# A hybrid conformer/Mamba-2 layer on one core: stores moved to the GpSimd queue, pair weights loaded wholly from GpSimd, memory pieces handed out by age

## The chip, the cores and the metric

The kernel runs on one core of one Trainium2 chip. The core has TensorE (PE in the profile) for matmuls, VectorE (DVE), ScalarE (ACT), GpSimd (POOL) and SyncE (SP). Each engine works through its own list of instructions in order, and waits at an instruction until the semaphores that it names have come. DMA transfers are issued by SP and by POOL here and run on 16 DMA engines. The metric is the device time of the core in microseconds; lower is better.

## The reference

One layer for two request groups that share weights: 1024 prompt tokens and 32 sample tokens, so 1056 columns in all. Everything is float32.

```
proj = x @ w_in + b_in                      # 1024 -> 11296 columns, split into nine parts
u = a_val * sigmoid(a_glu)                  # branch A: depthwise conv of width 31, layer norm, silu
out_a = (silu(layer_norm(conv31(u))) * silu(a_gate)) @ w_a_out
xbc = silu(conv4(xbc))                      # branch B: x/B/C through a depthwise conv of width 4,
y = ssd_scan(x, dt, A, B, C) + d_skip * x   #           chunked state-space scan, 4 groups of 8 heads
out_b = gated_rmsnorm(y, z) @ w_b_out
merged = sigmoid(g_a) * out_a + sigmoid(g_b) * out_b
x_new = layer_norm(2**0.25 * x + merged @ w_out + sigmoid(g_p) * (p @ w_ple))
```

The new caches (the last 30 and 3 rows of the two convolutions' inputs) and the final scan states are outputs too.

## The kernel before

All activations lie with channels on the 128 partitions and the 1056 tokens along the free dimension. Every matrix product is made of float32r halves: an operand is rounded to a high part by ACT (`..h`) and DVE subtracts to get the low part (`..l`), and three matmuls (high x low, low x high, high x high) give one product.

**Stages.** The work is written as numbered slots, and each slot as a list of named places (`ld0`, `ld`, `st`, `d0`, `a0`, `d1`, `a1`, `a2`, `pm`, `d2`, `pe`, `end`) at which functions registered with `at(slot, place, fn)` run. The order in which the program is written is the order on every engine; no scheduler moves anything.

- Before slot 1: loads, the products with `w_ple`, the `dt` products.
- *Pair slots* 1 to 27 (`pair_slot`): two 128-column tiles of `w_in` at once by a Strassen-like scheme with seven products j = 0 to 6, each 24 matmuls. In the text pair i (0 to 26) is slot i + 1. Its weights are seven 128x512 matrices `w{i}_0` to `w{i}_6`: sums of quarter matrices. A raw tile (`r11`, `r12`, `r22`, `s1`, `s2`, `s3`) is loaded, and for the sums further quarters are added into it by accumulating DMAs that only GpSimd issues (`pw_add`). `s2` gets two additions, is rounded for product 2 (`w{i}_2`), then gets a fourth quarter and is rounded again for product 5 (`w{i}_5`: this is the "S4" of the change). `prep_act(i, pos)` and `prep_dve(i, pos)` say after which product these steps are written. Between them DVE works off a queue of the 31-tap convolution (`run_fill`), as many taps as an estimate of its time allows (`dve[0]` against 2820 ns a product).
- *Classic slots* 28 to 61 (`S_CL` = 28): one 128-column tile of `w_in` each, 72 matmuls, and beside it one step of the state-space scan (`ssd_group`: transposes and products on PE, decay on ACT, carry and updates on DVE). Many tiles are spilled to DRAM and loaded back: `d_z`, `d_yn`, `d_ca`, `d_base`, `d_row`.
- Slots 62 to 77 (`S_OB`, product with `w_b_out`), 78 to 85 (`S_OA`, `w_a_out`), and from 86 (`S_WO`) the product with `w_out`, the last layer norm and the outputs.

**Memory pieces.** Tiles come from two pools of equal pieces, `T` (22 pieces, later more) and `U` (7 slightly longer ones). `tget` takes a piece of `T` if one is free and else one of `U`; `put` appends a piece at the end of its pool's list and `get` takes the head. A piece is put back when the program is written past its last use; the first writer of its next tile waits on the chip until the earlier tile's last reader, a store to DRAM among them, is done.

**Queues.** SP issues all loads and all stores (both through `load`, line 188, and four direct calls), POOL only the accumulating DMAs (line 471). Each DMA takes one of eight semaphores of its queue's kind in turn, so that a DMA may have to wait for the one eight places earlier. All operations of one kind on an engine are recorded at one helper's line: 171 tensor_tensor, 175 scalar_tensor_tensor, 185 activation, 191 matmul, 188 DMA from SP.

Of the kernel before, what the change touches and what calls it, by code (L numbers as in the profile page):

```python
# [102 lines left out]
class Units:  # L103


    def __init__(self, pool, n, cols, prefix):
        self.cols, self.n, self.prefix = cols, 0, prefix
        self.free = deque((pool, f"{prefix}{i}") for i in range(n))
        self.tag = {}

    def get(self, shape, dtype=F32, name="u"):
        assert self.free, f"out of units for {name}"
        tag = self.free.popleft()
        self.n += 1
# [14 lines left out]
def emit(nc, tc, I, O, ctx):  # L129
# [4 lines left out]
    T = Units(tpool, 22, 1064, "t")  # L134
    U = Units(tpool, 7, 1116, "u")
# [51 lines left out]
    def load(dst, src):  # L187
        nc.sync.dma_start(dst, src)  # L188

# [158 lines left out]
    def rstd_chain(get_v, scale, s, done):  # L348
# [21 lines left out]
        def move_row():  # L370
            load(d_row[i:i + 1, :], q["v"][0:1, :])
# [3 lines left out]
        def move_root():  # L375
            load(d_row[i + 1].rearrange("(p c) -> p c", p=96), sm(1))
# [1419 lines left out]
```

## Time and profile before

| | |
|---|---|
| median of 3 runs | 1672.31 us (1670.03 to 1672.37) |
| the profiled execution | 1677.25 us, its span 1675.5 us |
| busy over the span | PE 1541.6 us, DVE 1196.6, ACT 828.6, POOL 120.3 |
| pair slots | about 45 to 654 us |
| classic slots | about 654 to 1261 us |
| products with w_b_out and w_a_out | about 1261 to 1565 us |
| product with w_out, last norm | 1565 us to the end |

Times in the views are microseconds from the start of the span. In the view by stretches a row gives, for each engine, busy time and the number of instructions, then the mean clock granted to TensorE (1.00 is full speed), the busy share of the DMA engines and GB/s. "SPq" is SP issuing a DMA. In the chain of waits a row "DMA a<-b" is the time from a transfer's issue until it landed, where the next step of the chain waited for that landing. Groups carry the program's names with the buffer numbers left out, so `s<-in_w` is any raw `s` tile's load.

### The profile page before, as it was taken

To read this page: it belongs to the slowest core of one execution; us is meant where nothing else is said; L and a number is where in the kernel's file an instruction comes from. 1 tells how busy PE (TensorE), PEld (TensorE's weight loads), DVE (VectorE), ACT (ScalarE), POOL (GpSimd) and SP (SyncE) were. 2 spreads that over 40 slices of the span, in tenths; PEclk is the share of its full clock that TensorE was granted. 3 is DMA by queue.
4 is the path that set the end of the run, shared out by engine and by line. 5 is a ranking of instruction groups with operands and counts; after the bars stand their busy time and mean duration, and the time that the engine had idled before them with its cause. 6 is when DMAs were issued, how large, how long until landed. Compare 5 with 4: busy or idle time off the path is not lost.

```text
span 1675.5 us, 27209 instructions
## 1 busy us (share of the span) xinstructions
PE 1541.6 (92%) x10895; PEld 1487.5 (89%) x10895; DVE 1196.6 (71%) x1628; ACT 828.6 (49%) x1436; POOL 120.3 (7%) x148
## 2 busy tenths in 40 slices
PE   7888899999999998899979897779979999999997
PEld 7888899999999998799979796668969999999997
DVE  7757778888899977998866546545655568686654
ACT  7544343333333345676567566646756344343333
POOL 1211122222122210000000000000000000000000
PEclk9899999999999999999989998899999999999998
DMA  8787778778777862433354545235555546497422
GB/s 292 192 234 168 188 193 206 201 190 227 188 181 168 207 139 63 106 80 96 91 149 107 148 128 145 70 107 149 163 139 160 184 141 218 167 332 247 176 75 82
DMA packets 166205, 272.08 MB, mean 162 GB/s; under 512 B 31607, under 2 KB 87927, under 8 KB 166078
## 3 DMA queue, kind: packets, MB, share of 16 engines
q1 hardware_dynamic: 146638, 234.94, 44.4%
q0 software_dynamic: 19440, 35.40, 13.1%
q8 instruction: 85, 1.39, 0.3%
q14 instruction: 42, 0.34, 0.1%
HBM read 213.07 MB, written 57.22 MB: 161 GB/s over the span
## 4 chain that ended last, share of the span: by engine, by line
PE 61%; DVE 13%; DMA 13%; ACT 7%; issue 4%; SPq 2%; DVEq 0%; ACTq 0%
PE ps L191 60%; SPq L188 2%; DMA d_z<-zt_t 2%; DMA d_ca<-cat_t 2%; DMA d_base<-cb_t 2%; DVE cae_u L175 2%; DVE cao_u L175 2%; DMA out_conv_b<-vin_t 2%; DVE cb_t L175 1%; DMA d_yn<-cbo_t 1%; ACT L_t L185 1%; DMA d_ple<-pl 1%; DMA cw_u<-in_wo 1%; PE ps L974 1%; ACT L185 1%
## 5 line engine op out<-in xcount | busy, mean ns | idle before, releaser
L175 DVE SCALAR_TENSOR_TENSOR cae_u<-uin_u,par,cae_u 128x1086 f32<-128x1086 f32 x120 | 161.1, 1343 | 0.0
L471 POOL DMA_DIRECT2D s<-in_w x135 | 117.4, 997 | 494.1 <-DMA s<-in_w 162.1
L175 DVE SCALAR_TENSOR_TENSOR cao_u<-uin_u,par,cao_u 128x1086 f32<-128x1086 f32 x112 | 150.3, 1342 | 0.0
L185 ACT ACT_TABLE_LOAD x77 | 98.8, 1283 | 58.8 <-DMA d_yn<-cbo_t 24.2
L171 DVE TENSOR_TENSOR wlo<-wraw,whi 128x1024 fp32r<-128x1024 f32 x59 | 72.1, 1223 | 71.5 <-ACT whi L185 71.5
L191 PE MATMUL ps<-L_t,X 128*64 128x128 f32 (+1 forms) x528 | 40.0, 300 | 56.4 <-DVE ps L171 52.9
L191 PEld LDWEIGHTS ps<-L_t,X 128*64 128x64 f32 (+1 forms) x528 | 31.4, 152 | 64.2 <-DVE ps L171 55.7
L185 ACT ACTIVATE whi<-wraw 128x1024 fp32r<-128x1024 f32 x59 | 62.3, 1056 | 47.8 <-PE ps L191 28.3
L175 DVE SCALAR_TENSOR_TENSOR cb_t<-vin_t,par,cb_t 128x1059 f32<-128x1059 f32 x60 | 79.1, 1318 | 3.5 <-ACT cb_t L185 2.3
L175 DVE SCALAR_TENSOR_TENSOR cbo_t<-cbo_t,par,ps 128x128 f32<-128x128 f32 (+1 forms) x144 | 38.7, 331 | 57.2 <-PE ps L191 57.1
L185 ACT ACTIVATE gb_t<-ps,par 128x528 f32<-128x528 f32 x30 | 21.1, 702 | 117.7 <-PE ps L191 111.5
L185 ACT ACTIVATE L_t<-L_t,tk 128x128 f32<-128x128 f32 (+1 forms) x264 | 77.9, 381 | 0.0
L185 ACT ACTIVATE vin_t<-ps,par 128x352 f32<-128x352 f32 (+5 forms) x88 | 38.3, 471 | 62.2 <-PE ps L191 58.3
L191 PE MATMUL ps<-t3l,w_4h 128*128 128x264 f32 x216 | 62.9, 291 | 5.3 <-ACT sg_t L185 5.3
L191 PE MATMUL ps<-t3h,w_4l 128*128 128x264 f32 x216 | 62.9, 291 | 0.0
L171 DVE TENSOR_TENSOR M<-ps,mask 128x128 f32<-128x128 f32 (+1 forms) x36 | 9.9, 274 | 73.9 <-ACT B L185 73.3
L191 PE MATMUL ps<-t3h,w_4h 128*128 128x264 f32 x216 | 62.5, 289 | 0.0
L191 PE MATMUL ps<-n2l,w_2h 128*128 128x264 f32 x216 | 61.7, 286 | 0.2 <-ACT ga_t L185 0.2
L191 PE MATMUL ps<-n2h,w_2h 128*128 128x264 f32 x216 | 61.7, 286 | 0.0
L191 PE MATMUL ps<-t4h,w_6h 128*128 128x264 f32 x216 | 61.6, 285 | 0.0
L191 PE MATMUL ps<-n2h,w_2l 128*128 128x264 f32 x216 | 61.4, 284 | 0.0
L191 PE MATMUL ps<-t4l,w_6h 128*128 128x264 f32 x216 | 61.3, 284 | 0.0
(857 smaller groups left out, 5910.1 us busy)
## 6 DMA issues: line engine op xcount, KB each, us to landing
s<-in_w POOLq DMA_DIRECT2D x135, 256.0 KB, 5.7
r<-in_w SPq DMA_DIRECT2D x81, 256.0 KB, 4.1
s<-in_w SPq DMA_DIRECT2D x81, 256.0 KB, 3.5
wraw<-in_w SPq DMA_DIRECT2D x33, 512.0 KB, 5.7
L_t<-d_accp SPq DMA_DIRECT2D x29, 512.0 KB, 7.0
d_yn<-cbo_t SPq DMA_DIRECT2D x16, 528.0 KB, 8.0
yraw_t<-d_yn SPq DMA_DIRECT2D x16, 528.0 KB, 5.8
wraw<-in_wb SPq DMA_DIRECT2D x16, 512.0 KB, 3.7
```

The costliest lines, as they stand in the source:

```text
L171: nc.vector.tensor_tensor(out, a, b, op)
L175: nc.vector.scalar_tensor_tensor(out, a, s, b, op0, op1)
L185: nc.scalar.activation(out, a, f, **kw)
L188: nc.sync.dma_start(dst, src)
L191: nc.tensor.matmul(out, l, r, start=start, stop=stop, skip_group_check=more)
L471: nc.gpsimd.dma_start(pr[i, n], pw_src(i, (PARTS[n] + ("12",))[k]), accum_op=ALU.add)
L974: nc.tensor.transpose(pX[:nt, j * P:(j + 1) * P], XS[j][:, sl], ident)
```

## The change

1. `store(dst, src, *tiles)` replaces `load` for the stores. In slots below 28 it issues from SP as before; from slot 28 on it issues from GpSimd. It notes which tiles were stored, and puts them back.
2. All raw loads of pair weights (`pw_load`) are issued from GpSimd, in the same queue as the accumulating DMAs. The places in `prep_dve` are rearranged: the load of `s2` moves from position 0 to 3, its first addition from 3 to 5, and loads stand behind additions of the same position.
3. The second rounding of `s2` (product 5) moves: on ACT from position 0 to position 2, on DVE from position 0 to position 3. Product 5 itself stays where it was.
4. `Units` keeps for each free piece the slot in which it was put back, 1.5 slots later for one that was stored in that same slot, and `get` takes the piece with the smallest number. From slot 40 on `tget` compares the oldest of `T` with the oldest of `U`; before that `T` goes first as it did.

```diff
     def put(self, *ts):
         for t in ts:
-            self.free.append(self.tag.pop(id(t))[0])
+            (pool, tag), _ = self.tag.pop(id(t))
+            self.free.append((self.clock[0] + (1.5 if self.stored.pop(id(t), None) == self.clock[0] else 0.0), pool, tag))
     def get(self, shape, dtype=F32, name="u"):
-        tag = self.free.popleft()
+        k = min(range(len(self.free)), key=lambda i: (self.free[i][0], i))
+        _, pool, tag = self.free.pop(k)
...
     def tget(shape=(P, NT), dtype=F32, name="t"):
-        return (T if T.free else U).get(list(shape), dtype, name)
+        old = lambda x: min(f[0] for f in x.free) if x.free else 1e9
+        first = len(T.free) > 0 if cur[0] < S_CL + 12 else old(T) <= old(U)
+        return (T if first else U).get(list(shape), dtype, name)
...
+    def store(dst, src, *tiles):
+        (nc.sync if cur[0] < S_CL else nc.gpsimd).dma_start(dst, src)
+        for x in (T, U):
+            x.stored.update((id(t), cur[0]) for t in tiles)
+        tput(*tiles)
...
     def pw_load(i, n):
-            load(t, pw_src(i, PARTS[n][0]))
+            nc.gpsimd.dma_start(t, pw_src(i, PARTS[n][0]))
...
     def prep_act(i, pos):
-        if pos == 0:
-            pw_hi(i, 5, "s2")
-            pw_hi(i, 6, "r22")
         for j, n in {0: ((0, "r11"),), 2: ((1, "s1"),), 3: ((2, "s2"),), 4: ((3, "r12"),), 5: ((4, "s3"),)}.get(pos, ()):
             pw_hi(i + 1, j, n)
+        if pos == 0:
+            pw_hi(i, 6, "r22")
+        elif pos == 2:
+            pw_hi(i, 5, "s2")
     def prep_dve(i, pos):
         if pos == 0:
-            pw_lo(i, 5, "s2")
-            pw_load(i + 2, "s2")
...
         elif pos == 3:
+            pw_lo(i, 5, "s2")
             pw_lo(i + 1, 1, "s1")
             pw_load(i + 2, "s1")
-            pw_add(i + 2, "s2", 1)
+            pw_load(i + 2, "s2")
...
         elif pos == 5:
             pw_lo(i + 1, 3, "r12")
+            pw_add(i + 2, "s1", 1)
+            pw_add(i + 2, "s2", 1)
             pw_load(i + 2, "r12")
-            pw_add(i + 2, "s1", 1)
...
         def spill():
-            load(d_yn[4 * g + j], XSs[4 * g + j])
-            tput(XSs[4 * g + j])
+            store(d_yn[4 * g + j], XSs[4 * g + j], XSs[4 * g + j])
```

The other stores (`d_row`, `d_ca`, `d_z`, `d_wo`, `d_base`, `d_gate`, the convolution caches, the states) are replaced in the same way. The final output `y` and the stores of `d_ple`, `d_accp`, `d_expa` and `d_dec` stay on SP.

**Place 1: the queues in the middle of the pair slots.** On SP before, about pairs 9 to 11, a stretch in which weight loads (`r`, `s`), input tiles (`uin`, `bt`) and stores (`d_gate`, `d_base`) follow each other:

```order
L188 DMA s_9_2600<-in_w 128x512
L188 DMA uin_u_2604<-in_cache_a 128x30
L188 DMA bt_u_2633<-in_xT 128x1056
L188 DMA bt_u_2635<-in_xT 128x1056
L188 DMA d_gate<-ga_t_2357 128x1056
L188 DMA d_gate<-gb_t_2358 128x1056
L188 DMA s_10_2653<-in_w 128x512
L188 DMA r_10_2684<-in_w 128x512
L188 DMA r_9_2686<-in_w 128x512
```

The same stretch of SP after the change:

```order
L197 DMA uin_u_2604<-in_cache_a 128x30
L197 DMA bt_u_2633<-in_xT 128x1056
L197 DMA bt_u_2635<-in_xT 128x1056
L201 DMA d_gate<-ga_t_2357 128x1056
L201 DMA d_gate<-gb_t_2358 128x1056
L201 DMA d_base<-ga_t_2114 128x1056
L201 DMA d_base<-gb_t_2115 128x1056
L197 DMA bt_t_3121<-d_ple 128x1056
```

And POOL after the change, one pair slot of pair 18 (line 482 is a load, line 487 an addition; the name holds the pair for which the tile is):

```order
L487 DMA s2_19_4946<-in_w1 128x512
L487 DMA s3_19_5048<-in_w1 128x512
L482 DMA r11_20_5119<-in_w1 128x512
L482 DMA r22_19_5121<-in_w1 128x512
L482 DMA s1_20_5189<-in_w1 128x512
L482 DMA s2_20_5191<-in_w1 128x512
L487 DMA s2_19_4946<-in_w1 128x512
L487 DMA s1_20_5189<-in_w1 128x512
L487 DMA s2_20_5191<-in_w1 128x512
L482 DMA r12_20_5257<-in_w1 128x512
L482 DMA s3_20_5287<-in_w1 128x512
```

The six loads of a slot have left SP and stand among the five additions on POOL: eleven issues a slot where there were five.

**Place 2: DVE around the second rounding of `s2`,** pair 20. Before (`w20_5l` is the low part for product 5, `cao`/`cae` are taps of the convolution):

```order
L171 TENSOR_TENSOR w20_5l_5565<-s2_20_5092,w20_5h_5564 128x512
L175 SCALAR_TENSOR_TENSOR cae_u39_4949<-uin_u33_4073,par_74,cae_u39_4949 128x1086
L175 SCALAR_TENSOR_TENSOR cao_u40_5158<-uin_u33_4073,par_74,cao_u40_5158 128x1086
L171 TENSOR_TENSOR w20_6l_5568<-r22_20_5369,w20_6h_5567 128x512
L171 TENSOR_TENSOR w21_0l_5571<-r11_21_5367,w21_0h_5570 128x512
L175 SCALAR_TENSOR_TENSOR cae_u39_4949<-uin_u33_4073,par_74,cae_u39_4949 128x1086
L175 SCALAR_TENSOR_TENSOR cao_u40_5158<-uin_u33_4073,par_74,cao_u40_5158 128x1086
L175 SCALAR_TENSOR_TENSOR cae_u39_4949<-uin_u33_4073,par_74,cae_u39_4949 128x1086
L171 TENSOR_TENSOR w21_1l_5639<-s1_21_5432,w21_1h_5638 128x512
```

After:

```order
L184 SCALAR_TENSOR_TENSOR cae_u39_4948<-uin_u33_4073,par_74,cae_u39_4948 128x1086
L184 SCALAR_TENSOR_TENSOR cao_u40_5155<-uin_u33_4073,par_74,cao_u40_5155 128x1086
L180 TENSOR_TENSOR w20_6l_5568<-r22_20_5364,w20_6h_5567 128x512
L180 TENSOR_TENSOR w21_0l_5565<-r11_21_5362,w21_0h_5564 128x512
L184 SCALAR_TENSOR_TENSOR cae_u39_4948<-uin_u33_4073,par_74,cae_u39_4948 128x1086
L184 SCALAR_TENSOR_TENSOR cao_u40_5155<-uin_u33_4073,par_74,cao_u40_5155 128x1086
L184 SCALAR_TENSOR_TENSOR cae_u39_4948<-uin_u33_4073,par_74,cae_u39_4948 128x1086
L184 SCALAR_TENSOR_TENSOR cao_u40_5155<-uin_u33_4073,par_74,cao_u40_5155 128x1086
L180 TENSOR_TENSOR w20_5l_5636<-s2_20_5191,w20_5h_5635 128x512
L180 TENSOR_TENSOR w21_1l_5633<-s1_21_5431,w21_1h_5632 128x512
```

`w20_5l` now stands directly ahead of `w21_1l`, and one tap more than before stands ahead of that place, because the estimate that admits taps no longer counts the moved rounding there.

**Place 3: the queues in the classic slots,** about slots 49 and 50. SP before, with stores of scan results (`d_yn`), states and `cat` tiles between the loads:

```order
L188 DMA d_yn_97<-cbo_t106_7841 128x1056
L188 DMA d_yn_97<-cbo_t110_7994 128x1056
L188 DMA out_ssm<-hT_u53_8725 128x512
L188 DMA vin_t164_10534<-in_cache_b 128x3
L188 DMA L_t165_10537<-d_accp_100 128x8x128
L188 DMA wraw52_10539<-in_w1 128x1024
L188 DMA cat_u65_10541<-d_ca_99 128x1056
L188 DMA E2_2_10543<-d_expa_101 64x4x128 x2
L188 DMA d_ca_99<-cat_u64_10245 128x1056
L188 DMA d_yn_97<-cbo_t114_8149 128x1056
L188 DMA d_yn_97<-cbo_t118_8300 128x1056
L188 DMA out_conv_b<-vin_t157_10236 128x3 x2
```

The same stretch after the change, POOL:

```order
L201 DMA d_yn_97<-cbo_z106_7841 128x1056
L201 DMA d_yn_97<-cbo_t110_7994 128x1056
L201 DMA out_ssm<-hT_u53_8725 128x512
L201 DMA d_ca_99<-cat_u69_10245 128x1056
L201 DMA d_yn_97<-cbo_z114_8149 128x1056
L201 DMA d_yn_97<-cbo_z118_8300 128x1056
L201 DMA out_conv_b<-vin_y152_10236 128x3 x2
```

POOL holds nothing but stores there, and SP nothing but loads.

More of the change, by code (lines that the diff above doesn't have):

```diff
@@ L132, in emit @@
     dpool = ctx.enter_context(tc.tile_pool(name="scr", bufs=1, space=bass.MemoryType.DRAM))
-    T = Units(tpool, 22, 1064, "t")
-    U = Units(tpool, 7, 1116, "u")
+    cur = [0]
+    T, U = Units(cur), Units(cur)
+    T.add(tpool, [f"t{i}" for i in range(22)])
+    U.add(tpool, [f"u{i}" for i in range(7)])
     guards = [tc.tile_pool(name="x4", bufs=1), tc.tile_pool(name="pw", bufs=1, side="right")]
@@ L370, in move_row @@
         def move_row():
-            load(d_row[i:i + 1, :], q["v"][0:1, :])
+            store(d_row[i:i + 1, :], q["v"][0:1, :])
             load(sm(0), d_row[i].rearrange("(p c) -> p c", p=96))
@@ L375, in move_root @@
         def move_root():
-            load(d_row[i + 1].rearrange("(p c) -> p c", p=96), sm(1))
+            store(d_row[i + 1].rearrange("(p c) -> p c", p=96), sm(1))
             done(i + 1)
@@ L909, in spill @@
         def spill():
-            load(d_ca[t, :, :TP], acc[0][:, :TP])
-            load(d_ca[t, :, TP:], acc[0][:, WA - TS:])
-            U.put(acc[0])
+            store(d_ca[t, :, :TP], acc[0][:, :TP])
+            store(d_ca[t, :, TP:], acc[0][:, WA - TS:], acc[0])
         def later():
@@ L1033, in update @@
                 if i >= 7:
-                    at(cur[0] + 1, "st", lambda: load(O["ssm"][i - 7, :, 512 * g:512 * g + 512], hc))
+                    at(cur[0] + 1, "st", lambda: store(O["ssm"][i - 7, :, 512 * g:512 * g + 512], hc))
                 if i == 8:
@@ L1102, in away @@
         def away():
-            load(d_z[4 * g + j], zt)
-            tput(zt)
+            store(d_z[4 * g + j], zt, zt)
         def back():
@@ L1163, in cw_store @@
     def cw_store(m):
-        load(d_wo[m], cw[m])
-        tput(cw.pop(m))
+        t = cw.pop(m)
+        store(d_wo[m], t, t)
     def cb_sum(m, t):
@@ L1180, in cb_away @@
     def cb_away():
-        load(d_row[10:11, :], cb["S"][0:1, :])
-        tput(cb["S"])
+        store(d_row[10:11, :], cb["S"][0:1, :], cb["S"])
     def cb_back():
@@ L1195, in cb_store @@
     def cb_store(m):
-        load(d_base[m], cb[m])
-        tput(cb.pop(m))
+        t = cb.pop(m)
+        store(d_base[m], t, t)
         if m == 7:
@@ L1318, in ln_away @@
     def ln_away():
-        load(d_row[11:12, :], ln["S"][0:1, :])
-        tput(ln["S"])
+        store(d_row[11:12, :], ln["S"][0:1, :], ln["S"])
     def ln_back():
@@ L1326, in ca_away @@
     def ca_away(t):
-        load(d_ca[t], cat[t])
-        tput(cat[t])
+        store(d_ca[t], cat[t], cat[t])
     A0 = B - 17
@@ L1431, in gate_spill @@
     def gate_spill(gt, n):
-        load(d_gate[n], gt)
-        tput(gt)
+        store(d_gate[n], gt, gt)
     def base_tiles(s, ts, ns):
@@ L1463, in spill @@
             for t, m in zip(ts, ns):
-                load(d_base[m], t)
-                tput(t)
+                store(d_base[m], t, t)
         at(s + 1, "ld", fetch, lambda m: d_ple[m])
@@ L1536, in emit @@
     sp = spool.__enter__()
-    T.free.extend((t2pool, f"y{i}") for i in range(3))
+    T.add(t2pool, [f"y{i}" for i in range(3)], cur[0])
     new_psum("ps2")
@@ L1550, in emit @@
             t3pool = ctx.enter_context(tc.tile_pool(name="t3", bufs=1, side="right", reuse_waits="tile"))
-            T.free.extend((t3pool, f"z{i}") for i in range(10))
+            T.add(t3pool, [f"z{i}" for i in range(10)], cur[0])
         if kind == "z":
@@ L1590, in emit @@
             x2pool = ctx.enter_context(tc.tile_pool(name="x2", bufs=1, reuse_waits="tile"))
-            T.free.extend((x2pool, f"x{i}") for i in range(2))
+            T.add(x2pool, [f"x{i}" for i in range(2)], cur[0])
             banks[:] = [0, 1, 2, 3, 4]
```

32 lines of the change are left out of this document (15 added, 17 removed).

## The prediction

> **What bounds the kernel now.** I read the page's totals first, then the stretches, then the chain of waits. The totals name TensorE:
>
> ```profile
> span 1675.5 us, 27209 instructions
> PE 1541.6 (92%) x10895; PEld 1487.5 (89%) x10895; DVE 1196.6 (71%) x1628; ACT 828.6 (49%) x1436; POOL 120.3 (7%) x148
> PE 61%; DVE 13%; DMA 13%; ACT 7%; issue 4%; SPq 2%; DVEq 0%; ACTq 0%
> ```
>
> A busy PE can't be shortened by this change, which leaves every matmul in place. What it can shorten is the time in which PE waits or runs below full clock. The stretches show where that is (columns: length, then busy time and instructions of PE, PEld, DVE, ACT, POOL, then granted clock, DMA share, GB/s):
>
> ```profile
> 0.00:45.30 45.30, 35.43 (x192) 34.60 (x193) 32.29 (x51) 33.40 (x69) 5.37 (x15) 0.96 0.87 288
> 95.80:201.10 105.30, 89.64 (x683) 88.77 (x683) 73.42 (x96) 37.96 (x70) 17.41 (x20) 0.92 0.73 192
> 242.20:288.50 46.30, 43.27 (x339) 42.84 (x338) 40.57 (x50) 16.67 (x28) 9.89 (x12) 0.96 0.83 205
> 309.10:354.50 45.40, 42.99 (x337) 42.55 (x337) 39.67 (x48) 15.49 (x27) 9.80 (x12) 0.96 0.85 220
> 375.10:421.30 46.20, 43.20 (x338) 42.77 (x337) 40.53 (x50) 16.69 (x28) 9.91 (x12) 0.96 0.86 220
> 441.90:606.50 164.60, 164.60 (x1347) 164.60 (x1346) 148.93 (x177) 64.12 (x112) 34.78 (x40) 1.00 0.75 181
> 720.40:842.10 121.70, 121.70 (x835) 113.95 (x834) 107.77 (x142) 81.76 (x154) 0.00 (x0) 1.00 0.35 91
> 842.10:1261.10 419.00, 357.19 (x2325) 326.48 (x2325) 235.29 (x353) 262.86 (x467) 0.00 (x0) 0.92 0.47 131
> 1349.00:1535.00 186.00, 186.00 (x1158) 185.21 (x1159) 135.87 (x184) 74.42 (x81) 0.00 (x0) 1.00 0.61 218
> 1535.00:1565.30 30.30, 26.39 (x146) 25.86 (x145) 18.25 (x27) 10.68 (x14) 0.00 (x0) 0.89 0.50 181
> ```
>
> Each stage has an undisturbed stretch in which PE is always busy at clock 1.00. It gives a time per matmul: pair slots 164.60/1347 = 0.1222 us (a slot of 20.6 us), classic slots 121.70/835 = 0.1457 us (slots 32 to 39: 15.2 us each), the later products 186.00/1158 = 0.1606 us. What the other stretches take above that is their excess:
>
> - slots 40 to 61 (842 to 1261 us): 419.0 - 2325 x 0.1457 = **80.1 us**;
> - pairs 8-9, 11-12 and 14-15: 137.9 - 1014 x 0.1222 = **14.0 us**;
> - pairs 2 to 5: 105.3 - 683 x 0.1222 = **21.8 us**;
> - end of the w_a_out product: 30.3 - 146 x 0.1606 = **6.9 us**.
>
> So half of what can be won lies in slots 40 to 61. The chain of waits names what ends last there:
>
> ```profile
> 845.55 10.64 DMA d_yn<-cbo_t
> 918.07 10.55 DMA out_conv_b<-vin_t
> 1019.83 10.40 DMA d_yn<-cbo_t
> 1040.94 10.04 DMA d_ca<-cat_t
> 1068.25 8.40 DMA out_conv_b<-vin_t
> 1089.79 9.59 DMA d_ca<-cat_t
> 1114.25 9.66 DMA d_ca<-cat_t
> 1137.60 6.91 DMA out_conv_b<-vin_t
> 1204.63 10.46 DMA d_z<-zt_t
> 1218.20 9.96 DMA d_z<-zt_t
> 1237.87 10.62 DMA d_z<-zt_t
> ```
>
> Eleven stores. Nothing reads their result at that moment: each holds a memory piece that ACT, DVE or a load wants to overwrite. A piece stored in this slot was handed out again in this slot; the first writer waits out the 7 to 10.6 us of landing, ACT or DVE stands still behind it, and the scan's products find their PSUM not ready:
>
> ```profile
> PE ps L191 <- DVE ps L171: 61.8, 10, 10.9
> ```
>
> Asked for the stretch 617 to 1350 us alone, the view gives the same row: all ten waits lie there.
>
> **Part 1: stores on POOL and pieces by age.** Both old and new rule hand out a free piece by its age; what differs is the 1.5 slots added to a stored piece, the use of U, and when the store is issued. I followed both rules through the kernel's own requests. In slots 40 to 61 either version asks for 110 pieces that were used before. Before, 19 of them had been put back by a store in the same slot, and 14 in the slot before; now it is 1 and 4, and 32 of the stored ones have rested two or three slots. With a slot of 15.2 us a landing of 10.6 us is then over. Besides, on SP such a store is issued only after the loads ahead of it, and those wait for pieces too; on POOL only stores stand ahead of it.
>
> What it adds: one POOL issue a store, off every path as long as POOL keeps up. POOL's issue of a plain 4224-byte-row store isn't in the trace; the nearest rows are the accumulating loads:
>
> ```profile
> L471 POOL DMA_DIRECT2D s<-in_w x71 | 61.7, 1025 | 240.8 <-DVE w_2l L171 61.9 <-DMA s<-in_w 58.7 <-DVE w_0l L171 24.5
> 459.25 2.65 POOL L471 DMA_DIRECT2D s<-in_w  x3 [6.11 <-DVE w_2l L171]
> s<-in_w POOLq DMA_DIRECT2D x135, 256.0 KB, 5.7
> s<-in_w SPq DMA_DIRECT2D x81, 256.0 KB, 3.5
> ```
>
> About 1 us, so at most six in a slot of 15.2 us; I take it at nothing, since POOL does nothing else there. If that cover were gone a store would issue a slot late, which the resting pieces absorb. Bounds of the gain: 0 if the landings are merely awaited elsewhere, 80 us if none is left. ACT's 262.9 us and DVE's 235.3 us in these 419 us fit into the 339 us that PE needs, so no other engine takes over. I take 85%, **-68 us**: one same-slot piece stays, and pieces put back by plain readers in the same slot (8 before, 10 now) still make short waits.
>
> The Trainium skill speaks against this: "DMA: Bandwidth & Descriptors", section "Issuing engines are not separate DMA queues", says that starting DMAs from several engines only saves the sequencer's time for issuing them. By that rule alone the move is worth SP's issue time on the chain, rival B below. [...]
>
> The same mechanism ends the w_a_out product (chain: `d_base<-cb_t` landings before `w_out` can be split); of 6.9 us I take **-5 us**, bounds 0 and -6.9.
>
> **Part 2: pair weights from POOL.** SP loses six issues a slot. In pair 11 a load of `bt` stood behind the `s3` load, which waits for DVE, and DVE then waited for `bt`:
>
> ```profile
> 310.88 0.33 SPq L188 DMA_DIRECT2D s<-in_w  x1
> 311.94 1.31 SPq L188 DMA_DIRECT2D bt_u<-in_xT  x2
> 318.50 1.26 DVE L175 SCALAR_TENSOR_TENSOR ga_t<-bt_u,ga_t 128x1056 f32<-128x1056 f32 x1 [5.66 <-DMA bt_u<-in_xT]
> DVE ga_t L175 <- DMA bt_u<-in_xT: 16.9, 3, 5.7
> 116.31 11.31 DMA cw_u<-in_wo
> ```
>
> The three waits of 16.9 us cause the 14.0 us. After the change only tiles and stores are ahead of `bt`; its pieces are free well before in two of the pairs, and in pair 11 only since late in the slot before. I take **-9 us** (bounds 0 and -14). In pairs 2 to 5 the `cw` loads are late in the same way (11.31 us on the chain), but these 4 MB still have to pass beside the weights at a DMA share of 0.73; of 21.8 us I take **-9 us** (bounds +5 and -18).
>
> POOL then issues 11 a slot: at 0.88 us (2.65/3) to 1.03 us that is 9.7 to 11.3 us of 20.6. In its order `s2`'s chain is the longest. In pair 17 (from 441.9 us) these rows set its ends:
>
> ```profile
> 452.02 0.62 ACT L185 ACTIVATE w_2h<-s 128x512 fp32r<-128x512 f32 x1
> 454.42 0.68 DVE L171 TENSOR_TENSOR w_1l<-s,w_1h 128x512 fp32r<-128x512 f32 x1
> 456.62 0.28 PE L191 MATMUL ps<-x4l_t,w_5h 128*128 128x264 f32 x1
> ```
>
> The load is issued after DVE's rounding, about 15 us into the slot; landed 3.5 to 5.7 us later; first addition at 20; landed 5.7 us later; second addition at about 26, landed at 32, which is 11 us into the next slot, where ACT rounds it at 10 us (452.02). So ACT may wait 1 to 2 us, and PE needs `s2`'s product not before the third of the slot after: **0**.
>
> **Part 3: rounding later.** PE needs the low part when product 5 begins, at 456.62 in pair 17. Pair 0:
>
> ```profile
> 66.28 0.68 DVE L171 TENSOR_TENSOR w_5l<-s,w_5h 128x512 fp32r<-128x512 f32 x1
> 69.26 0.63 ACT L185 ACTIVATE w_1h<-s 128x512 fp32r<-128x512 f32 x1
> ```
>
> In pair 17 `w_5l` takes the place of `w_1l`, which ended at 455.10, and one tap more is ahead of it (1.26 us, less the 0.60 us of `w_5l`'s own former place): 455.8, still 0.9 us before PE. That is thin, but in the undisturbed slots it holds. By the same reckoning from their own rows pairs 7, 10 and 13 miss by 0.9 us each, and pairs 8, 11 and 14 would miss by 4 to 5 us if the `bt` wait stayed. Pair 0 loses for certain: PE waited there for `w_5l`, whose subtraction began at 66.28; now ACT rounds it after `w_1h` (69.26), so it comes at 71 in place of 67: +4 us. And at the start POOL's weight loads run against the input tiles, 1 MB earlier at 288 GB/s (first row above): up to +4, taken as +1. In all **+8 us** (bounds +3 and +20).
>
> **The sum.** 1675.5 - 68 - 5 - 9 - 9 + 8 = 1592.5 us of span. The profiled execution took 1677.25 us, 1.75 more than its span, and lies 4.9 above the median of the runs, 1672.31. So 1592.5 + 1.75 - 4.9 = **1589 us**, rounded to 1590.
>
> **Rivals.**
>
> A. *The waits move and half stays.* Landings grow under two queues, or the next thing in line (ACT's decay, a load waiting for a piece) takes up half: -34 in place of -68, so 1623 us. For it: 46 plain pieces are still reused after at most one slot (50 before), and no trace shows a store from POOL. Against it: slots 32 to 39 run at 15.2 us with much the same work of ACT and DVE. 17%.
>
> B. *Only issue time is won.* SPq is 2% of the whole chain, 34 us, and these slots hold most of it: at best some 30 us in place of 68, the rest unchanged but for part 3: 1675.5 - 30 + 8, by the same steps 1650 us. Against it: the eleven landings, 107 us of chain, are the pieces' and not SP's. 5%.
>
> C. *The pair slots get worse:* the pairs gain nothing and part 3 costs its 20: 1675.5 - 68 - 5 + 20, 1619 us. For it: the thin margin. 10%.
>
> D. *POOL becomes the bound (slower).* Place: the pair slots, where one queue in order now holds loads and the additions that wait for them. It decides once eleven issues with their waits exceed 20.6 us, 1.87 us each. At 2.2 us a slot takes 24.2, +3.6 us for 25 slots, 90 us, which eats all the rest: 1675.5 - 83 + 90, 1679 us. Against it: 0.88 to 1.03 us now. 6%.
>
> That the change doesn't do what it says is excluded by the count of 19 to 1.
>
> **How the numbers follow.** Forecast 62%, with a range of its own of 1570 to 1612. The range reaches up to A and C and down to all bounds but the last few: 1560 to 1635. A difference under 0.2% can't be told from none here. Faster by more: 0.62 + 0.17 + 0.05 + 0.10 = 0.94, of which I take off 0.02 for mixtures; same 0.02; slower 0.06.
>
> **What would show it.** Right: no store landing of 8 us or more on the chain between 842 and 1170 us, that stretch at clock 0.97 or more, about 15.7 us a slot; DVE's wait for `bt` under 6 us; POOL's share near 20%. Wrong in part 1: `DMA d_yn`, `d_ca` or `d_z` on the chain again. Wrong in part 2: ACT waiting for `s<-in_w` or `r<-in_w` by tens of us. Wrong in part 3: PE waiting for `w_5l` more than 20 us in all.

## The result, and the profile after

The changed kernel takes 1589.94 us (median of four runs, 1587.43 to 1592.33) against 1671.17 us (1667.63 to 1672.37) for the kernel before, run on the same chip: a ratio of 0.9517 with a 95% interval of 0.9495 to 0.9539. Its profiled execution has a span of 1587.3 us. The views are of one execution each, and that of the kernel before, 1677.25 us, lies 6 us above the median of 1671.17: the spans differ by 88.2 us where the medians differ by 81.2, so the differences by stretch below come to some 7 us too much in all.

The first rows of the page of the changed kernel, with the granted clock by fortieths of the span (in tenths of full speed) and the engines of the chain of waits:

```profile
span 1587.3 us, 27345 instructions
PE 1521.2 (96%) x10895; PEld 1472.0 (93%) x10895; DVE 1196.9 (75%) x1628; ACT 831.7 (52%) x1436; POOL 275.2 (17%) x423
PEclk9899999999999999999999999999999999999999
PE 60%; issue 17%; DVE 10%; DMA 7%; ACT 3%; POOL 1%; SPq 1%; POOLq 0%; DVEq 0%; ACTq 0%
```

PE has the same 10895 matmuls and is busy 20 us less, since the clock granted to it fell less often: in the rows by stretch below it is 0.98 to 1.00 where PE is busy for 96% of the time or more, and 0.90 to 0.95 where PE is busy for 75 to 91%. The matmuls were not touched, so all of the 88 us of span is waiting and clock.

The view by stretches shows where the 88 us lie. The kernel before, with the bounds of the stretches set at the first product of pair 0, of pair 6, of slot 28 and so on:

```profile
45.30:201.10 155.80, 133.64 (x1020) 132.35 (x1019) 109.96 (x145) 63.84 (x117) 30.66 (x36) 0.92 0.74 190
201.10:653.70 452.60, 440.63 (x3531) 439.15 (x3530) 382.40 (x455) 179.88 (x305) 84.24 (x97) 0.98 0.73 183
1535.00:1570.90 35.90, 29.96 (x171) 28.96 (x170) 22.20 (x33) 11.18 (x15) 0.00 (x0) 0.90 0.58 208
```

The changed kernel, the same stretches and the start:

```profile
0.00:51.20 51.20, 38.35 (x192) 36.74 (x193) 33.19 (x51) 33.99 (x69) 10.27 (x24) 0.93 0.78 264
51.20:193.80 142.60, 130.04 (x1019) 128.67 (x1019) 111.12 (x147) 64.41 (x117) 50.06 (x71) 0.95 0.80 218
193.80:630.40 436.60, 432.74 (x3529) 432.55 (x3529) 380.34 (x453) 180.47 (x305) 156.18 (x221) 1.00 0.73 186
820.80:1180.70 359.90, 345.96 (x2328) 318.41 (x2326) 235.36 (x353) 265.22 (x469) 30.70 (x57) 0.99 0.55 150
1456.30:1483.50 27.20, 26.63 (x170) 26.17 (x169) 21.04 (x30) 9.74 (x13) 2.13 (x4) 1.00 0.61 212
```

| stretch | before | after | difference |
|---|---|---|---|
| start, to pair 0's first product | 45.3 | 51.2 | +5.9 |
| pairs 0 to 5 | 155.8 | 142.6 | -13.2 |
| pairs 6 to 26 | 452.6 | 436.6 | -16.0 |
| slots 40 to 61 | 419.0 | 359.9 | -59.1 |
| end of the w_a_out product | 35.9 | 27.2 | -8.7 |
| all the rest (88.2 less the sum above) | | | +2.9 |

The eleven store landings of 7 to 10.6 us are gone from the chain between 820 and 1181 us. In their place stand these (chain of the changed kernel; start, us, what), and, in the view of waits (us in total, times, longest), DVE's wait for `E`, the tile of decay factors that the scan loads from `d_expa`:

```profile
867.48 1.60 DMA d_row<-zt_u
872.00 7.85 DMA E<-d_expa
1012.99 1.60 DMA d_row<-zt_y
1017.31 8.21 DMA E<-d_expa
1159.93 1.60 DMA d_row<-zt_y
1166.39 9.30 DMA E<-d_expa
```

```profile
DVE ps L180 <- DMA E<-d_expa: 31.3, 11, 6.3
PE ps L207 <- DVE ps L180: 13.9, 4, 4.5
ACT w_2h L194 <- DMA s<-in_w: 20.4, 8, 5.1
```

DVE waited 5.9 us in all for `E` before and waits 31.3 us now; PE's waits for DVE in these slots fell from 61.8 to 13.9 us, and all four that are left are behind `E`. They lie in slots 50, 52, 59 and 61 (22, 24, 31 and 33 counted from slot 28, as the expectations count them), which take 21.6, 18.5, 20.0 and 20.3 us where their like take 15.4 to 16.4. So the stage was freed of one wait and got a smaller one, and the first question for the runs is which half of part 1 did which.

### The profile page after: what moved, and what is told of

It is laid out like the page before. It is cut to its first block, busy times and chain, and to the rows that moved or that the text cites. A ratio compares the mean times of both kernels' runs of the same rounds, so it can differ in the third digit from the quotient of the medians.

```text
span 1587.3 us, 27345 instructions
## 1 busy us (share of the span) xinstructions
PE 1521.2 (96%) x10895; PEld 1472.0 (93%) x10895; DVE 1196.9 (75%) x1628; ACT 831.7 (52%) x1436; POOL 275.2 (17%) x423
## 4 chain that ended last, share of the span: by engine, by line
PE 60%; issue 17%; DVE 10%; DMA 7%; ACT 3%; POOL 1%; SPq 1%; POOLq 0%; DVEq 0%; ACTq 0%
PE ps L207 60%; DMA E<-d_expa 2%; DMA s<-in_w 1%; DVE cao_u L184 1%; DVE cb_t L184 1%; DVE cae_u L184 1%; DMA wq<-in_wp 1%; SPq L197 1%; DVE cb_z L184 1%; DMA d_wo<-cw_t 1%; PE ps L990 1%; DMA xraw_t<-in_xT 0%; DVE cb_u L184 0%; DVE dt_u L184 0%; DMA cw_z<-in_wo 0%
## 5 line engine op out<-in xcount | busy, mean ns | idle before, releaser
L487 POOL DMA_DIRECT2D s<-in_w x135 | 120.4, 909 | 195.6 <-DMA s<-in_w 145.6
L482 POOL DMA_DIRECT2D s<-in_w x81 | 45.2, 558 | 142.5 <-issue 54.3
L482 POOL DMA_DIRECT2D r<-in_w x81 | 59.0, 761 | 46.8 <-DVE w_0l L180 31.9
L184 DVE SCALAR_TENSOR_TENSOR cbo_z<-cbo_z,par,ps 128x128 f32<-128x128 f32 (+1 forms) x81 | 24.6, 331 | 50.3 <-PE ps L207 50.3
L207 PE MATMUL ps<-t4l,w_6h 128*128 128x264 f32 x216 | 61.8, 286 | 0.0
L207 PE MATMUL ps<-t4h,w_6l 128*128 128x264 f32 x216 | 61.5, 285 | 0.0
L194 ACT ACTIVATE ga_t<-ps,par 128x528 f32<-128x528 f32 x32 | 22.5, 702 | 67.5 <-PE ps L207 67.5
L180 DVE TENSOR_TENSOR acc_t<-acc_t,ps 128x352 f32<-128x352 f32 x63 | 31.1, 516 | 35.0 <-PE ps L207 34.9
L180 DVE TENSOR_TENSOR ps<-ps,E 128x512 f32<-128x512 f32 (+1 forms) x32 | 20.6, 643 | 32.6 <-DMA E<-d_expa 31.3
```

The source lines that it names most:

```text
L180: nc.vector.tensor_tensor(out, a, b, op)
L184: nc.vector.scalar_tensor_tensor(out, a, s, b, op0, op1)
L194: nc.scalar.activation(out, a, f, **kw)
L207: nc.tensor.matmul(out, l, r, start=start, stop=stop, skip_group_check=more)
L482: nc.gpsimd.dma_start(t, pw_src(i, PARTS[n][0]))
L487: nc.gpsimd.dma_start(pr[i, n], pw_src(i, (PARTS[n] + ("12",))[k]), accum_op=ALU.add)
```

## The experiments

All are edits of the changed kernel. Times are medians of four runs, with the ratio to the kernel before, measured beside them.

### Which half of part 1 does it: the queue or the age rule?

Three of the four kernels of this set put back one half or both. Stores from SP again:

```diff
-        (nc.sync if cur[0] < S_CL else nc.gpsimd).dma_start(dst, src)
+        nc.sync.dma_start(dst, src)
```

> The changed kernel with every store issued from SP again; pieces are still handed out by age, pair weights still come from GpSimd. The theory of the prediction (the stored piece's rest is what counts, the queue little): the landing of a store falls into the slots in which its piece rests, whichever queue started it, so slots 40 to 61 stay near 16 us each; SP again has four to six stores in a slot at 0.3 to 0.6 us and waits for what they wait for, some 10 to 15 us in all: about 1602 us. The rival (the queue is what counts: loads stood behind stores on SP): the 59 us of slots 40 to 61 and the 8 us at the end of the w_a_out product come back, about 1655 us, with ACT or DVE waiting for loads that stand behind a store.

Pieces by the old rule:

```diff
-        k = min(range(len(self.free)), key=lambda i: (self.free[i][0], i))
+        k = 0
...
-        first = len(T.free) > 0 if cur[0] < S_CL + 12 else old(T) <= old(U)
+        first = len(T.free) > 0
```

> The changed kernel with the old rule for pieces (first back, first out, one group before the other); stores stay on GpSimd. The theory of the prediction (rest counts): 19 stored pieces are handed out again in the same slot, the first writer waits 5 to 8 us of landing, and most of the gain in slots 40 to 61 is gone: about 1640 us, with landings of d_yn, out_conv_b, d_ca and d_z on the chain of waits again. The rival (the queue counts): a store from GpSimd is issued as soon as its data is there, since nothing stands ahead of it, and lands in 5.2 us in place of 8.0 (medians of d_yn in the two traces), so at most 15 us come back: about 1603 us.

Both edits together:

> The changed kernel with both halves of part 1 undone (stores from SP, old rule for pieces); parts 2 and 3 stay. By the sum of the two traces, slots 40 to 61 lose their 59 us again and the end of the w_a_out product its 8: 1590 + 67 = about 1657 us, 14 us below the kernel before. If the two halves of part 1 do the same work twice, each of the two kernels that keeps one half lies much nearer to 1590 than to this; if both are needed, both lie near to this.

The fourth has part 1 alone: `pw_load` through `load` again, `prep_act` and `prep_dve` as before the change.

> Part 1 alone: stores from GpSimd in the second half and pieces by age; pair weights are loaded from SP and rounded at the old places. By the traces it gains the 59 + 8 us of part 1 and none of the 14 that parts 2 and 3 gained together in the pair slots: 1671 - 67 = about 1604 us. The pair slots then show again 14 us of loss in pairs 8 to 15 (DVE waiting for bt) and 21.8 in pairs 2 to 5, and the start is again 5.9 us earlier. If the two parts help each other (SP's stores of the pair slots are not moved), it comes out apart from this by more than 5 us.

| | us | ratio, interval | slots 40 to 61 | end of w_a_out |
|---|---|---|---|---|
| both halves (the change) | 1589.94 | 0.9517 [0.9495, 0.9539] | 359.9 | 27.2 |
| age rule, stores on SP (e1) | 1577.42 | 0.9432 [0.9411, 0.9453] | 350.1 | 26.6 |
| old rule, stores on GpSimd (e2) | 1603.08 | 0.9577 [0.9552, 0.9602] | 363.3 | 40.0 |
| neither (e3) | 1656.05 | 0.9893 [0.9871, 0.9915] | 418.2 | 37.5 |
| part 1 alone (e4) | 1604.82 | 0.9580 [0.9551, 0.9608] | 359.3 | 26.1 |

The rows behind the middle column, of e1, e2 and e3 in this order:

```profile
820.00:1170.10 350.10, 342.80 (x2328) 316.95 (x2326) 235.49 (x353) 262.36 (x466) 0.00 (x0) 1.00 0.57 153
```

```profile
820.00:1183.30 363.30, 347.45 (x2325) 319.59 (x2325) 236.03 (x354) 265.39 (x469) 30.61 (x57) 0.98 0.54 153
```

```profile
820.20:1238.40 418.20, 356.88 (x2327) 325.92 (x2326) 235.33 (x353) 263.86 (x469) 0.00 (x0) 0.92 0.47 132
```

The last two expectations came out to within 1 us. The second came out at its rival's number, the first 25 us below the lower of its two: I had set "rest" against "queue" as if one had to fall, and each alone removes most of the wait (68.1 us of the stage by age, 54.9 us by the queue). They are two cures for one illness. The kernel with neither shows it whole (e3 at the turn from slot 49 to 50; rows of DVE, SP and ACT, then of the chain):

```profile
987.65 1.25 DVE L180 TENSOR_TENSOR cbo_t<-cbo_t,zt_y 128x1056 f32<-128x1056 f32 x1
987.79 0.33 SPq L197 DMA_DIRECT2D vin_z<-in_cache_b  x1
992.49 0.37 SPq L197 DMA_DIRECT2D L_y<-d_accp  x1
994.85 2.60 SPq L197 DMA_DIRECT2D E<-d_expa  x2
998.41 0.43 SPq L201 DMA_DIRECT2D d_yn<-cbo_t  x1
1008.66 1.28 ACT L194 ACT_TABLE_LOAD   x1 [13.11 <-DMA d_yn<-cbo_t]
998.41 10.16 DMA d_yn<-cbo_t
```

DVE is done with `cbo_t` at 988.9. The store stands on SP behind loads that wait for buffers of their own, and behind the issue of `E`, and is issued at 998.4, 9.5 us later; it lands 10.2 us after that, and ACT has by then waited 13.1 us to write into the piece. So the piece is held for 19.7 us, and only half of that is the transfer. With the old rule and stores on GpSimd the same store:

```profile
968.08 1.25 DVE L180 TENSOR_TENSOR cbo_t<-cbo_t,zt_y 128x1056 f32<-128x1056 f32 x1
969.74 0.53 POOL L201 DMA_DIRECT2D d_yn<-cbo_t  x1 [1.81 <-DVE cbo_t L180]
```

It is issued 0.4 us after DVE, and the piece, though handed out just as soon, is clean before ACT comes to it. With the age rule and stores on SP the stores are issued nearly as late (at the same turn some 9 us after DVE in e1), but the pieces are not wanted for another slot or two; one exception is left, in slot 45, where ACT waits 6.9 us for a store of `out_conv_b`. At the end of the w_a_out product only the age rule helps: with the old rule the stretch takes 40.0 and 37.5 us, whichever queue stores.

And the two together are 12.5 us worse than the age rule alone. That is the second question.

### Why stores on GpSimd cost 12 us once pieces rest

At the turn from slot 49 to 50 the changed kernel shows this on POOL, SP and DVE:

```profile
970.76 0.53 POOL L201 DMA_DIRECT2D d_yn<-cbo_z  x1 [1.80 <-DVE cbo_z L180]
971.93 0.53 POOL L201 DMA_DIRECT2D d_yn<-cbo_z  x1 [0.64 <-DVE cbo_z L180]
972.56 1.17 POOL L201 DMA_DIRECT2D out_conv_b<-vin_y  x2
975.42 3.69 SPq L197 DMA_DIRECT2D cat_u<-d_ca  x1
979.16 2.43 SPq L197 DMA_DIRECT2D E<-d_expa  x2
992.06 0.70 DVE L180 TENSOR_TENSOR ps<-ps,E 128x512 f32<-128x512 f32 x1 [6.31 <-DMA E<-d_expa]
```

and the kernel with its stores on SP (e1), at the same place:

```profile
981.16 0.38 SPq L197 DMA_DIRECT2D cat_u<-d_ca  x1
981.59 2.72 SPq L197 DMA_DIRECT2D E<-d_expa  x2
984.42 0.67 SPq L201 DMA_DIRECT2D d_ca<-cat_u  x1
985.14 1.23 SPq L201 DMA_DIRECT2D d_yn<-cbo_z  x2
991.32 0.70 DVE L180 TENSOR_TENSOR ps<-ps,E 128x512 f32<-128x512 f32 x1
```

On SP the loads of a slot stand ahead of its stores, and `E`, which DVE wants 7 to 10 us later, goes first. On GpSimd the stores go out as soon as their data is there, some 8 us ahead of `E`, whose issue then takes longer to come through (`cat_u` before it 3.69 in place of 0.38 us) and whose transfer runs beside theirs. A second way in which `E` could be late is that SP stands still: it waits for GpSimd's store of the root's row before it reads it back. Two kernels tell these apart. One issues `E` a slot earlier:

```diff
-            at(s0 + i + 1, "ld", load_e)
+            at(s0 + i, "ld", load_e)
```

> The changed kernel with the scan's load of E issued one slot earlier (it has two buffers; nothing else moves). With stores on SP the kernel took 1577, 12 us less than with stores on GpSimd, and the difference lies in the slots 22, 24, 31 and 33 of the second half, where DVE waits for E. Theory: on SP the loads of a slot stood ahead of its stores; on GpSimd the stores start first and share the DMA engines with E, whose landing grew from 8.5 to 10.2 us in the first of these slots. With E a slot earlier the four waits, 13.9 us of PE standing still, go: about 1576 us. Rival: SP itself is held up behind the read of the root's row, which waits for GpSimd's store; then E is late in two of the four slots only because everything on SP is, the weights and L too, and an earlier E helps in the other two: about 1583 us.

The other reads the row back from GpSimd:

```diff
-            load(sm(0), d_row[i].rearrange("(p c) -> p c", p=96))
+            (nc.sync if cur[0] < S_CL else nc.gpsimd).dma_start(sm(0), d_row[i].rearrange("(p c) -> p c", p=96))
```

> The changed kernel with the read of the root's row (root_t<-d_row) issued from GpSimd, behind the store that it waits for, in place of SP; E stays where it was. Theory of the shared DMA engines: slots 24 and 33 are hardly better, since E still meets the stores: 1587 to 1591 us. Rival of the blocked SP: in those two slots L, the weights and E are no longer held up, 6 to 8 us less: about 1583 us.

With `E` early: **1572.03 us**, 0.9391 [0.9358, 0.9424]. With the row on GpSimd: **1582.19 us**, 0.9453 [0.9419, 0.9486]. Slots 40 to 61 of the first, then of the second:

```profile
822.20:1165.00 342.80, 340.98 (x2328) 315.72 (x2326) 235.22 (x353) 262.03 (x466) 30.09 (x56) 1.00 0.56 157
```

```profile
822.40:1178.80 356.40, 345.75 (x2328) 318.89 (x2326) 235.62 (x353) 262.83 (x466) 32.17 (x60) 0.99 0.55 153
```

The first came out 4 us below its expectation, the second at its rival's number. `E` is the carrier: issued early, it leaves 342.8 us for the stage, 1.8 above PE's busy time, and no wait of DVE for it. With the row on GpSimd slots 59 and 61 drop from 20.0 and 20.3 us to 16.1 and 16.4 (in the six kernels that are alike in this stage, the change, e4 and e7 to e10, these two take 17.5 to 21.1 us). So there it is enough that SP no longer stands still behind the row. The rows of the changed kernel for slot 61 (POOL's store, and SP's read of it, for which SP had waited 23.2 us):

```profile
1159.93 0.50 POOL L201 DMA_DIRECT2D d_row<-zt_y  x1 [18.87 <-ACT zt_y L194]
1161.55 0.33 SPq L197 DMA_DIRECT2D root_t<-d_row  x1
```

That SP stands still is not new with GpSimd's stores, though: with its stores on SP (e1) it waits 14.8 and 13.4 us at these two places for the row's data, and `E` is in time. What e1 does not have is stores ahead of `E`. In the changed kernel GpSimd issues two `d_yn` 6 to 7 us ahead of it for slot 59 and a `d_z` 3 us ahead in slot 61; in e1 both follow it. So the stores that run ahead fit all four slots, and in 59 and 61 a free SP can issue `E` early enough all the same.

Slots 50 and 52 don't gain from the row on GpSimd (21.1 and 23.1 us). I had expected the blocked SP in slots 52 and 61; it was 59 and 61. In slot 52 of the changed kernel SP does wait 16.3 us for the row, but with the row on GpSimd other loads ahead of `E` wait too, `E` is issued only 1 us earlier in the slot, and its two halves then take 14.1 and 12.6 us to land in place of 10.7 and 8.8. How much of the lateness in slot 50 is the slower issue and how much the slower transfer is not told apart; the slow issue is not `cat_u`'s own, since with the row on GpSimd `cat_u` takes 0.49 us there and the issues of `E` behind it 5.62 in place of 2.43.

### Parts 2 and 3

Loads of pair weights from SP, rounding at the new places:

```diff
-            nc.gpsimd.dma_start(t, pw_src(i, PARTS[n][0]))
+            load(t, pw_src(i, PARTS[n][0]))
```

> The changed kernel with the six loads of pair weights a slot on SP again, rounded at the new places. Together with the run in which part 1 stands alone (loads on SP and rounded early, 1605) and the changed kernel (loads on GpSimd and rounded late, 1590) it tells parts 2 and 3 apart. Theory of the prediction: part 2 carries the gain, part 3 costs: the wait for bt and the late cw loads are back (+18 and more), the start is 5.9 us earlier: about 1603 us, or 1610 where the thinner margin meets the bt wait. Rival: the later rounding carries it (s2's buffer and GpSimd's order): about 1584 us, since the start is won back.

Loads from GpSimd, `prep_act` and `prep_dve` as before the change:

> The changed kernel with the rounding of the last two parts, and so the order of loads and additions, at the old places; the loads still come from GpSimd. It closes the square of parts 2 and 3: loads on SP and rounded early 1605, on SP and late 1608, on GpSimd and late 1590. Theory (part 3 is a small cost everywhere, and the loads on GpSimd carry the whole gain of 15 to 18 us): about 1586 us, pair 0 one or two us shorter and the 2.9 us wait for w_5l in pair 4 gone. Rival (on GpSimd the loads need the later rounding, since the old order puts a load that waits for DVE's rounding at the slot's start ahead of the additions on the same queue): ACT waits for s<-in_w by tens of us, 1597 us or more.

With part 1 alone (e4) and the change itself these make a square; all four have part 1:

| loads from, rounding | us | ratio, interval | start | pairs 0 to 5 | pairs 6 to 26 |
|---|---|---|---|---|---|
| SP, early (e4) | 1604.82 | 0.9580 [0.9551, 0.9608] | 44.8 | 153.2 | 452.2 |
| SP, late (e8) | 1607.72 | 0.9596 [0.9564, 0.9628] | 45.2 | 152.8 | 446.8 |
| GpSimd, early (e9) | 1587.94 | 0.9493 [0.9454, 0.9533] | 52.2 | 137.6 | 440.1 |
| GpSimd, late (the change) | 1589.94 | 0.9517 [0.9495, 0.9539] | 51.2 | 142.6 | 436.6 |

The times of e9 run from 1582.39 to 1592.72 us, and its stretches are of an execution of 1583.47, so they show it at its best. The queue of the loads carries the gain, about 17 us; the late rounding makes either pair of kernels 2 to 3 us slower, which the intervals don't tell from nothing. So e8 came out between the two values of its first expectation, and e9 2 us above its own; there pair 0 is 4.3 us shorter, not one or two. From SP, DVE waits for `bt` as before, in e4:

```profile
DVE ga_t L184 <- DMA bt_u<-in_xT: 18.2, 3, 6.8
```

a row that has no counterpart once the loads are on GpSimd. The late rounding does have a use, if a small one: with the early one ACT waits for the last addition into `s2`,

```profile
ACT w_2h L194 <- DMA s<-in_w: 64.8, 24, 8.1
```

64.8 us in e9 against 20.4 in the changed kernel, and one of these waits reaches PE (pair 11, 23.2 in place of 20.5 us).

**The start.** The five loads of pair 0 from SP, behind the input tiles:

```diff
     for n in ("r11", "s1", "s2", "r12", "s3"):
-        pw_load(0, n)
+        t = pr[0, n] = raw_tile(n, f"{n}_0")
+        load(t, pw_src(0, PARTS[n][0]))
```

> The changed kernel with only the five first weight loads of pair 0 on SP, behind the input tiles, as before the change. Theory: the 5.9 us by which pair 0 began later (45.3 to 51.2 us) come from 1 MB of weights that runs beside the input tiles; they go: about 1584 us, pair 0 at 45 to 46 us. Rival: the start is later because GpSimd issues the later loads (r22, r11 of the next pair) late or because of the second rounding; then it stays at 51 us and 1590.

**1585.93 us**, 0.9474 [0.9446, 0.9503], 4 us below the change with intervals that just overlap; pair 0 begins at 45.4 us:

```profile
0.00:45.40 45.40, 35.33 (x192) 33.91 (x193) 32.43 (x51) 33.39 (x69) 7.63 (x19) 0.94 0.87 299
```

So the late start is that 1.3 MB of weights, which on GpSimd have nothing ahead of them and run beside the input tiles; in the changed kernel the chain of the first 30 us is `praw`, `xraw` and `wq` landing, the last after 14.81 us. Of the 5.8 us that are won, pairs 0 to 5 take 1.5 back. (The prediction and the expectation counted 1 MB; five tiles of 256 KB are 1.3.)

**Pair 0.** Second rounding of `s2` at the old place for pair 0 only:

```diff
-        elif pos == 2:
-            pw_hi(i, 5, "s2")
+        if pos == (2 if i else 0):
+            pw_hi(i, 5, "s2")
```

(and `pw_lo` the same way).

> The changed kernel with s2's second rounding at the old place in pair 0 alone. The prediction gave this 4 us (w_5l at 67 in place of 71 us); in the traces PE waits 8.0 us for w_5h in pair 0 and waited 6.5 us before the change, so the later rounding is worth 1.5 us at most and most of the wait is for DVE, which is at work on dt: about 1588.5 us. If the prediction's 4 us were right: about 1586 us.

**1588.08 us**, 0.9485 [0.9461, 0.9508]: the time came out as expected, though 1.9 us is less than the intervals can tell from nothing, and it came about in another way. Pairs 0, 1 and 2 of the changed kernel, then of this one:

```profile
51.20:82.60 31.40, 23.08 (x170) 22.35 (x170) 25.21 (x37) 14.29 (x23) 12.57 (x17) 0.89 0.58 140
82.60:103.50 20.90, 20.81 (x170) 20.60 (x170) 10.34 (x14) 11.62 (x24) 5.59 (x8) 1.00 0.98 291
103.50:124.00 20.50, 20.50 (x170) 20.50 (x169) 16.09 (x26) 10.85 (x24) 7.81 (x11) 1.00 0.95 288
```

```profile
51.80:78.20 26.40, 22.48 (x169) 22.06 (x169) 22.43 (x34) 14.41 (x23) 9.86 (x14) 0.94 0.61 152
99.20:124.10 24.90, 22.34 (x171) 22.13 (x170) 16.77 (x28) 10.83 (x24) 9.44 (x15) 0.93 0.97 286
```

Pair 0 is 5 us shorter, so the prediction's 4 us for it were about right, and pair 2 gives 4.4 back. In pairs 1 and 2 the DMA engines are busy at 0.95 to 0.98, and the load and two additions of pair 3's `s2` land one after the other in 6.8, 7.2 and 7.7 us, where the median of such a transfer over the kernel is 4.9. ACT waits 8.0 us for the last in pair 2, and PE 2.6 us for the `uin` that stands behind it in ACT's list. That the busy DMA engines set this pace is likely, and no run shows it alone.

### All together

`E` early, the start on SP and pair 0 rounded early, once with the stores on SP and once on GpSimd:

> The changed kernel with what the runs so far point to: stores on SP again, E a slot earlier, pair 0's first five weight loads on SP, and its second rounding of s2 at the old place. From the run with E early (1572): minus 4 for the start as measured, minus 1 for pair 0: 1567 us. On the stores' queue the theory (the stores' harm is E's lateness alone) expects no difference from the next kernel beyond 3 us; the rival (SP's loads stand behind stores too) expects it 6 us or more slower than that.

> The same with the stores on GpSimd as in the changed kernel: 1567 us. If stores on GpSimd still harm something other than E, it is 6 us or more slower than the kernel before in this row; if SP's order is the worse once E is early, it is faster.

Both had been expected at 1567. Stores on SP: **1571.76 us**, 0.9387 [0.9366, 0.9409]. Stores on GpSimd: **1564.43 us**, 0.9347 [0.9327, 0.9368], the fastest of all, 25.5 us below the change. The three edits alone had given 17.9, 4.0 and 1.9 us, 23.8 together. The 7.3 us between the two is the rival of the first expectation: with its stores on SP slot 45 takes 22.1 us in place of 15.4, by these rows (start, us, SP's issue; then ACT's instruction and what ended its wait):

```profile
893.52 1.60 SPq L201 DMA_DIRECT2D out_conv_b<-vin_t  x2
901.05 1.18 ACT L194 ACTIVATE cbo_t<-cb_z 128x1024 f32<-128x1024 f32 x2 [6.95 <-DMA out_conv_b<-vin_t]
```

A store again, late behind loads that wait for their pieces, and one piece that did not rest long enough; it is the one that e1 shows in slot 45 (19.8 us there). With the stores on GpSimd the same store is issued at 876.2 us, 17 us earlier. With the stores on GpSimd slots 40 to 61 take 342.8 us, at a clock of 1.00:

```profile
814.10:1156.90 342.80, 341.00 (x2327) 315.74 (x2325) 235.14 (x353) 262.00 (x466) 30.08 (x56) 1.00 0.56 156
```

## Why the prediction was right, and where it was not

The time (1590 against 1589.94) is closer than its terms deserve. Against a span of 1675.5 the sum gave 1592.5; measured are 1587.3, an error of 5.2 us. It vanished in the last step, from span to median: the sum took off 4.9 us, by which the execution before lay above its median, while the execution after lies 0.9 us below its own. That the two errors cancel is luck.

| term | forecast | measured |
|---|---|---|
| part 1, slots 40 to 61 | -68 (0 to -80) | -59.1 |
| part 1, end of w_a_out | -5 (0 to -6.9) | -8.7 |
| part 2, `bt` | -9 (0 to -14) | -12.1 (pairs 6 to 26, e4 to e9) |
| part 2, `cw` in pairs 2 to 5 | -9 (+5 to -18) | -15.6 (pairs 0 to 5, e4 to e9) |
| part 3, pair 0 | +4 | +5.0 (pairs 0 to 5, e9 to the change) |
| part 3, margins in pairs 7, 10, 13 | +2.7 | -3.5 (pairs 6 to 26, e9 to the change) |
| start | +1 (up to +4) | +5.9 |

- **The mechanism of part 1** was right: the landings left the chain, the piece is what ACT and DVE waited for, and the age rule alone is worth 68.1 us of the stage, the very number taken (by 85% of an excess; that the two agree to the decimal is luck). The rest of stored pieces is the whole of the gain, and GpSimd's queue was not needed for it.
- **The step that failed in part 1** is the cost of the queue: "one POOL issue a store, off every path as long as POOL keeps up. [...] I take it at nothing". POOL kept up, and the stage still lost 9.8 us (350.1 to 359.9). I priced the issue and not what the order had been good for: on SP a slot's stores could not start before its loads. With -68 us the stage would have had 351.0 us, 16.0 a slot; it has 16.4. (The 15.7 a slot among the signs does not follow from the sum.)
- **Rival B and the rule of the Trainium skill** ("DMA: Bandwidth & Descriptors", "Issuing engines are not separate DMA queues"). It says that DMAs interleave on the same 16 DMA engines whichever engine starts them, and that several issuers save only the time of issuing. The first half fits what `E` shows here: it lands late when GpSimd's stores start first. The landings themselves were not alike on the two queues, though: the median of a `d_yn` store is 8.0 us from SP in the kernel before and 5.2 from GpSimd in the changed one. The second half does not hold for this kernel: with the old rule for pieces, GpSimd's queue removes 54.9 us of the stage, more than all of SP's 34 us of issue on the chain of the whole kernel before, since a store's issue was held 9.5 us by what stood ahead of it in line.
- **Which queue for a plain transfer.** Stores on SP are 12.5 us better than on GpSimd while `E` is tight (e1), and 7.3 us worse once it is early (e11 and e12); the plain loads of pair weights are some 17 us better on GpSimd (e4 and e9). The Trainium skill ("DMA: Bandwidth & Descriptors", section "SWDGE vs HWDGE vs iDMA") gives plain transfers to SP or ACT throughout; the runs agree in the first of the three cases only. The same section of the Trainium skill also says that a DMA engine goes round its internal queues and that the two kinds of issue feed different ones. A store from GpSimd would then take its turns beside a load that it would stand behind on one queue; the late `E` agrees with that, and no run here proves it.
- **Rival A** (the waits move, half stays) named the right kind of event in the wrong size: 13.9 of 61.8 us of PE's waits moved to `E`, a load that the prediction does not name (DVE waited 5.9 us for it before).
- **Part 2** was right in direction and under-sized in both terms, though inside its bounds: I took 9 of 14.0 and 9 of 21.8 us, and these stretches gave 12.1 and 15.6. The sign that I named against it, ACT waiting for `s<-in_w` by tens of us, did come (20.4 us), and was no sign of a net loss. Five of the eight waits, 14.5 us, lie in pairs 6 to 26, whose slots keep their 20.5 us; one of 4.6 us in pair 2 stands on the chain, behind landings of 4.5, 5.5 and 8.3 us, and pair 3 takes 22.8 us after it (29.8 before).
- **The end of the w_a_out product** went past its bound of 6.9 us because the stretch measured here is longer: the first 146 matmuls lose their whole excess (30.3 us before, 23.5 after for 148), and the rest, which the sum left out, goes from 5.6 to 3.7 us.
- **Part 3.** Pair 0's 4 us are there (4.3 in e9, 5.0 in e10), but in e10 pair 2 took 4.4 of them back. The 0.9 us misses of pairs 7, 10 and 13 did not appear: the view of waits has one wait of PE for `w_5l`, 2.9 us, in pair 4. Nor do they appear in e8, where `bt` is late as it was before, so the reckoning was off by more than that 0.9 us there, and why is open. Its other half came true in kind in e8, where the late rounding meets the late `bt`: PE waits for `w_5l` in pairs 8, 11 and 14, though 2.2, 1.8 and 2.9 us and not 4 to 5.
- **The start** was mis-sized: "up to +4, taken as +1" turned out +5.9, past the bound. The prediction counted 1 MB; 1.3 MB at 288 GB/s are 4.5 us. The load that is last, `wq`, lands 14.8 us after its issue; what the other 1.4 us are is open.
- **C and D** fell: of the pair slots only 0 and 4 grew by more than half a microsecond while all of them together shrank by 29.2, and POOL's share is 17%, its issues 0.56 to 0.91 us, far from the 1.87 at which it would have decided.

So errors of +8.9 (the queue's cost), +4.9 (start), -18 (pairs), -4 (w_a_out) and +3 (the rest) met in the span, and the step to the median gave back the 5 us that were left over.

## What to carry to other kernels

A memory piece is held from the last write until its store has landed, and the store's place in line can be half of that: give such a piece a slot of rest, or the store a queue of its own, and measure each alone before adding them. A queue that mixes loads and stores is also a priority, and moving stores out of it lets them overtake the loads of the next step, so move the tightest load ahead in the same edit. At the start, the order on one queue protects the first tiles that are needed; loads that are not urgent belong behind them.

## What the hardware showed that I had not expected

- Two cures of one wait, 68 and 55 us alone in a stage, gave 59 together, because the second lets stores start ahead of `E` and makes it late: in slot 50 `cat_u`'s issue ahead of it on SP took 3.69 us in place of 0.38 while GpSimd's stores were on their way.
- TensorE's granted clock in slots 40 to 61 went from 0.92 to 0.99, and PE's busy time there from 357.2 to 346.0 us with as many matmuls: some 11 of the 59 us are clock, won back by standing still less. With neither half of part 1 (e3) it is 0.92 and 356.9 again.
- In pairs 1 and 2 the DMA engines are busy at 0.95 to 0.98 with 272 to 291 GB/s; there, in e10, 4.4 of the 5.0 us by which PE was ahead were paid back within two pairs.
